# Low parts of the gate product's weights in a decoder block: ScalarE writes the negated high part, a transfer from DRAM adds the raw weights

## The chip, the core and the metric

The kernel runs on one core of a Trainium2 chip. The core has a matrix engine (TensorE, PE in the profile, with its weight loads as PEld), three engines for elementwise work (VectorE = DVE, ScalarE = ACT, GpSimd = POOL), SyncE (SP), which issues transfers, and 16 DMA engines. Each engine works through its own queue of instructions in order and waits on semaphores for the others. The metric is the device time of one execution in microseconds; smaller is better.

## The reference

The reference is one decoder block over 512 tokens of width 1024: two parallel branches (a short gated convolution and an mLSTM in chunks) from one wide input projection, a gated merge, an output projection, and at the end a gate with a per-layer embedding and a last normalisation. What matters here is the end:

```python
        merged = jax.nn.sigmoid(ga) * ya + jax.nn.sigmoid(gb) * yb
        x = x + jnp.einsum('bsd,de->bse', merged, w_o[l])

        gate = jax.nn.sigmoid(jnp.einsum('bsd,de->bse', rmsnorm(x, g_ple[l]), w_ple_gate[l]))
        x = x + gate * jnp.einsum('bsp,pd->bsd', p[l], w_ple[l])
    return rmsnorm(x, g_final)
```

The product with `w_ple_gate` (1024 x 1024, float32) is the gate product. It is the last large product of the kernel.

## The kernel before

**Precision.** Every large product is made of three: each float32 operand is cut into a high part (the operand rounded to the matrix engine's float32r format) and a low part (the operand less its high part, also in float32r), and `mm3` adds high x high (L233), high x low (L234) and low x high (L235) in PSUM. For weights, one operand is a tile of 128 x 4 x 512 numbers (2048 per partition, 1 MB). It lies raw in a tile `wraw` (four buffers), loaded by SyncE, and is cut in two halves (h = 0, 1) of 128 x 1024 each into the tiles `whi` and `wlo`. These have two buffers for each half, so that one operand can be cut while another is in use. In the profile a matmul's two inputs are named with the moving one first: `mm<-wlo,h` multiplies a low part of the weights.

**The list of operands.** `operands` lists the weight tiles in the order of their use, each with the sums that are to be made after its split: many of the kernel's products are made in Strassen's way with seven products in place of eight, and the sums of raw tiles that this needs are made by transfers that POOL issues (`add_chunk`, L156), which add a piece of DRAM weights to a raw tile in SBUF. The output projection `w_o` is such a product. The gate product is not: its four operands (two column halves n, two row halves) are the last four of the list, appended by the loop over `block(w_pg_v, ...)`, and no sum follows their split.

**The order of the work.** The order on TensorE, ScalarE, VectorE and GpSimd is that in which the code is written out. `next_operand` hands out the next operand and queues the split of the one after it; `tick`, called after each block of 12 or 24 matmuls, takes one half from that queue and calls `split_half`. So an operand's halves are cut while the operand ahead of it is in use. In `split_half` ScalarE writes the high part (L180) and VectorE subtracts it from the raw tile (L181). What a `tick` emits stands in ScalarE's and VectorE's queues behind the work of the blocks before.

**The end.** The last seven-product stage (`w_o`) runs until 795.7 us of the span. Its results are added to the residual, squared for the norm (`esq`, L1287), turned by TensorE (`ptk`, L1248) and cut (`h`, L240 and L241 or L243 and L244). Then the gate product runs in this order: first operand with token tiles 2 and 3, second operand with 2, 3, 0 and 1, first operand again with 0 and 1 (all for the first 512 columns; `gate_embedding` takes each finished tile through the sigmoid `e`, the product with the embedding and the residual `xr`, and POOL multiplies the result by the last norm's weights, `xg`, L1337). For the other 512 columns `last_part` uses the third operand with tiles 0 and 1, the fourth with 0 and 1, and then both with tiles 2 and 3. What follows each finished tile there is a long run of small steps on ScalarE, VectorE and POOL up to the output.

Of the kernel before, what the change touches and what calls it, by code (L numbers as in the profile page):

```python
# [9 lines left out]
F32 = mybir.dt.float32  # L10
F32R = mybir.dt.float32r
AF = mybir.ActivationFunctionType
ALU = mybir.AluOpType
# [23 lines left out]
def hybrid_block(ctx, tc, x, p, g_mix, w_in, conv_w, conv_b, w_a_out, b_gates, g_head,  # L37
                 w_b_out, w_o, g_ple, w_ple_gate, w_ple, g_final, out):
    nc = tc.nc
    act, dve, pool, pe = nc.scalar, nc.vector, nc.gpsimd, nc.tensor  # L40
# [28 lines left out]
    chunks, operands = [], []  # L69
# [10 lines left out]
    def block(view, pieces, halves=(0, HC)):  # L80
        for k0 in halves:
            operands.append((chunk(view, k0, pieces), []))
# [38 lines left out]
    for j, u in enumerate((b11, b21, b11, b22, b11, b12, b11)):  # L121
        for g in range(2):
# [4 lines left out]
    begun = {sums: o12}  # L127
    operands.extend([(o11, []), (sums, [(sums, o22, None)]), (o21, [(o12, o22, None)]), (sums, [(sums, o21, None)]),
                     (o22, []), (o12, []), (sums, [])])
    for n in range(2):  # L130
        block(w_pg_v, [(n * CW, CW)])

# [21 lines left out]
    def add_chunk(to, c, ks):  # L154
        for src, _, cs in chunks[c]:
            nc.gpsimd.dma_start(raws[to][:, ks, cs], src[:, ks, :], accum_op=ALU.add)  # L156
# [14 lines left out]
    def split_tiles(i, h):  # L171

        parts = [wsplit.tile([P, HH, CW], F32R, name=f"w{u}{i}{h}", tag=f"w{u}{h}", align_bytes=256)
                 for u in ("hi", "lo")]
        splits.setdefault(i, []).append(parts)
        return raws[operands[i][0]][:, HH * h:HH * h + HH, :], *parts

    def split_half(i, h, e_lo=None):
        t, hi, lo = split_tiles(i, h)
        act.activation(hi, t, AF.Copy)  # L180
        (e_lo or dve).tensor_tensor(lo, t, hi.bitcast(F32), ALU.subtract)  # L181
        ks = slice(HH * h, HH * h + HH)
        for to, c, eng in operands[i][1]:
            if eng is not None:
                eng.tensor_tensor(raws[to][:, ks, :], raws[to][:, ks, :], raws[c][:, ks, :], ALU.add)
            else:
                add_chunk(to, c, ks)
        if h == 1:
            done(i)

    def done(i):
        for c in [c for c in raws if last_use[c] == i]:
            del raws[c]
        load_free()
# [7 lines left out]
    def next_operand(follow=True):  # L202

        i = state["use"]
        state["use"] += 1
        while pieces:
            split_half(*pieces.popleft())
        if follow:
            queue_split()
        got = splits.pop(i)  # L210
        return [[got[kt // HH][u][:, kt % HH, :] for kt in range(HC)] for u in range(2)]
# [4 lines left out]
    def tick():  # L216
        new = [g for g in fresh if not next(g, True)]
        fresh.clear()
        if pieces:
            split_half(*pieces.popleft())  # L220
        active[:] = [g for g in active if not next(g, True)] + new
# [354 lines left out]
    def quarter(q):  # L576
        hi, lo = (u[:, q % HH, :] for u in splits[0][q // HH])
        return hi, lo, raws[0][:, q, :]
# [6 lines left out]
    hi, lo, raw = quarter(0)  # L585
# [47 lines left out]
    for t in range(2):  # L633
        keep_ple(t, 1, pss[t])

    split_half(1, 0, pool)
    for k in range(3):
        turn_x(k)
# [6 lines left out]
    for g in range(2):  # L645
        src = wg_raw[:, :, g * NH:(g + 1) * NH]
# [808 lines left out]
```

## Time and profile before

| | |
|---|---|
| time, median of 3 runs | 852.58 us (847.28 to 853.58) |
| the profiled execution, its own time | 851.58 us |
| its span, first to last instruction | 849.8 us |
| TensorE busy | 837.7 us (99%) |
| weight loads busy | 729.8 us (86%) |
| VectorE busy | 649.8 us (76%) |
| ScalarE busy | 498.1 us (59%) |
| GpSimd busy | 209.0 us (25%) |
| moved by DMA | 172.83 MB, mean 203 GB/s |
| transfers queued by POOL | 70.33 MB, 44.7% of the 16 engines' span |
| transfers queued by SP and ACT | 101.72 MB, 36.0% of the 16 engines' span |

Times inside the kernel are given in microseconds from the start of the span. A row of a timeline reads: start, duration, engine, line of the code, instruction, what it writes and reads, shape, count, and in brackets how long the engine had stood idle before it and what ended that. Matmuls are pipelined: a row shows 0.39 us, and one starts every 0.23 us. A row of the chain of work gives start, length, engine and line. A row of busy time by stretch gives the stretch, its length, busy time and number of instructions of TensorE, of the weight loads, of VectorE, ScalarE and POOL, the clock that TensorE was granted (1 is full speed), the share of the DMA engines that was busy, and GB/s. A row of the waits gives who waited for whom, us in total, times, and the longest.

### The profile page before, as it was taken

To read this page: it belongs to the slowest core of one execution; us is meant where nothing else is said; L and a number is where in the kernel's file an instruction comes from. 1 tells how busy PE (TensorE), PEld (TensorE's weight loads), DVE (VectorE), ACT (ScalarE), POOL (GpSimd) and SP (SyncE) were. 2 spreads that over 40 slices of the span, in tenths; PEclk is the share of its full clock that TensorE was granted. 3 is DMA by queue.
4 is the path that set the end of the run, shared out by engine and by line. 5 is a ranking of instruction groups with operands and counts; after the bars stand their busy time and mean duration, and the time that the engine had idled before them with its cause. 6 is when DMAs were issued, how large, how long until landed. Compare 5 with 4: busy or idle time off the path is not lost.

```text
span 849.8 us, 12141 instructions
## 1 busy us (share of the span) xinstructions
PE 837.7 (99%) x4602; PEld 729.8 (86%) x4602; DVE 649.8 (76%) x876; ACT 498.1 (59%) x726; POOL 209.0 (25%) x204
## 2 busy tenths in 40 slices
PE   9999999999999999999999999999999999999996
PEld 7888888888889988888888999999998887888885
DVE  5786767976787667788668779797885787899565
ACT  6467665667765576565776555545443355667543
POOL 5103122203124321220222333342410222122031
PEclk9999999999999999999999999999999999999998
DMA  9748769779968997896998799999989489799502
GB/s 316 266 139 177 163 135 222 196 267 238 266 127 207 245 223 166 200 219 208 256 230 212 161 213 181 183 182 182 182 276 375 83 199 275 195 250 228 191 0 100
DMA packets 103355, 172.83 MB, mean 203 GB/s; under 512 B 5564, under 2 KB 46064, under 8 KB 102016
## 3 DMA queue, kind: packets, MB, share of 16 engines
q0 software_dynamic: 39488, 70.33, 44.7%
q1 hardware_dynamic: 59792, 94.64, 33.7%
q10 hardware_dynamic: 4016, 7.08, 2.3%
q8 instruction: 36, 0.59, 0.3%
q14 instruction: 23, 0.19, 0.1%
HBM read 155.25 MB, written 16.78 MB: 202 GB/s over the span
## 4 chain that ended last, share of the span: by engine, by line
PE 93%; DMA 2%; DVE 2%; issue 1%; ACT 1%; SPq 0%; POOL 0%; POOLq 0%; ACTq 0%; DVEq 0%
PE mm L235 28%; PE mm L234 28%; PE mm L233 28%; DMA wraws<-in_w_b_out 2%; PE pv L233 1%; PE pv L235 1%; PE pv L234 1%; PE pty L816 1%; DMA xin<-in_x 1%; PE sc L235 1%; PE sc L234 1%; PE sc L233 1%; PE ptk L1248 0%; PE pth L1129 0%; PE pt L553 0%
## 5 line engine op out<-in xcount | busy, mean ns | idle before, releaser
L181 DVE TENSOR_TENSOR wlo<-wraw,whi 128x1024 fp32r<-128x1024 f32 x244 | 299.5, 1229 | 113.3 <-ACT whi L180 112.9
L180 ACT ACTIVATE whi<-wraw 128x1024 fp32r<-128x1024 f32 x246 | 257.2, 1054 | 109.6 <-PE mm L235 54.8
L156 POOL DMA_DIRECT2D wraw<-in_w_in x112 | 136.9, 1424 | 336.0 <-DVE wlo L181 231.1
L349 ACT ACTIVATE s<-mm 128x512 f32<-128x512 f32 x84 | 50.2, 597 | 98.1 <-PE mm L235 96.8
L233 PE MATMUL mm<-whi,hs 128*128 128x512 f32 x256 | 99.9, 390 | 0.0
L234 PE MATMUL mm<-wlo,hs 128*128 128x512 f32 x256 | 99.8, 390 | 0.0
L235 PE MATMUL mm<-whi,hs 128*128 128x512 f32 x256 | 99.7, 389 | 0.0
L233 PE MATMUL mm<-hn_hi,whi 128*128 128x256 f32 (+1 forms) x304 | 93.4, 307 | 0.0
L235 PE MATMUL mm<-hn_hi,wlo 128*128 128x256 f32 (+1 forms) x304 | 92.9, 306 | 0.0
L234 PE MATMUL mm<-hn_lo,whi 128*128 128x256 f32 (+1 forms) x304 | 92.9, 306 | 0.0
L233 PE MATMUL mm<-hs,whi 128*128 128x256 f32 x320 | 90.9, 284 | 0.0
L234 PE MATMUL mm<-hs,whi 128*128 128x256 f32 x320 | 90.5, 283 | 0.0
L235 PE MATMUL mm<-hs,wlo 128*128 128x256 f32 x320 | 90.5, 283 | 0.0
L234 PE MATMUL mm<-wlo,hn_hi 128*128 128x512 f32 x192 | 75.0, 391 | 0.0
L233 PE MATMUL mm<-whi,hn_hi 128*128 128x512 f32 x192 | 74.9, 390 | 0.0
L235 PE MATMUL mm<-whi,hn_lo 128*128 128x512 f32 x192 | 74.7, 389 | 0.0
L234 PEld LDWEIGHTS mm<-hs,whi 128*128 128x128 f32 x320 | 61.4, 192 | 0.0
L233 PEld LDWEIGHTS mm<-hs,whi 128*128 128x128 f32 x320 | 61.4, 192 | 0.0
L235 PEld LDWEIGHTS mm<-hs,wlo 128*128 128x128 f32 x320 | 61.4, 192 | 0.0
L235 PEld LDWEIGHTS mm<-hn_hi,wlo 128*128 128x128 f32 x304 | 58.1, 191 | 2.7 <-POOL wlo L181 0.2
L234 PEld LDWEIGHTS mm<-hn_lo,whi 128*128 128x128 f32 x304 | 58.1, 191 | 2.4
L233 PEld LDWEIGHTS mm<-hn_hi,whi 128*128 128x128 f32 x304 | 58.1, 191 | 2.4
(349 smaller groups left out, 1679.0 us busy)
## 6 DMA issues: line engine op xcount, KB each, us to landing
wraw<-in_w_in SPq DMA_DIRECT2D x32, 1024.0 KB, 5.5
wraw<-in_w_in POOLq DMA_DIRECT2D x52, 512.0 KB, 8.1
wraw<-in_w_in SPq DMA_DIRECT2D x48, 512.0 KB, 5.3
wraw<-in_w_in POOLq DMA_DIRECT2D x60, 256.0 KB, 5.9
wraw<-in_w_b_out SPq DMA_DIRECT2D x7, 1024.0 KB, 5.2
wraw<-in_w_b_out POOLq DMA_DIRECT2D x12, 512.0 KB, 6.5
wraw<-in_w_o SPq DMA_DIRECT2D x5, 1024.0 KB, 7.6
yt_d<-yc POOLq DMA_DIRECT2D x4, 1024.0 KB, 4.9
```

Source lines behind the costliest of these rows:

```text
L156: nc.gpsimd.dma_start(raws[to][:, ks, cs], src[:, ks, :], accum_op=ALU.add)
L180: act.activation(hi, t, AF.Copy)
L181: (e_lo or dve).tensor_tensor(lo, t, hi.bitcast(F32), ALU.subtract)
L233: pe.matmul(ps, lhsT=a[0], rhs=b[0], start=first, stop=False, **kw)
L234: pe.matmul(ps, lhsT=a[0], rhs=b[1], start=False, stop=False, **kw)
L235: pe.matmul(ps, lhsT=a[1], rhs=b[0], start=False, stop=last, **kw)
L349: act.activation(to[i], src, AF.Copy, scale=scale)
L816: pe.transpose(pts[v][:, t * P:(t + 1) * P], y[:, t, v * P:(v + 1) * P], ident)
```

## The change

```diff
@@ operands, in order of use
                      (o22, []), (o12, []), (sums, [])])
+    first_pg = len(operands)
     for n in range(2):
         block(w_pg_v, [(n * CW, CW)])

@@ split_half
         t, hi, lo = split_tiles(i, h)
         act.activation(hi, t, AF.Copy)
-        (e_lo or dve).tensor_tensor(lo, t, hi.bitcast(F32), ALU.subtract)
         ks = slice(HH * h, HH * h + HH)
+        if i >= first_pg:
+            act.activation(lo, hi.bitcast(F32), AF.Copy, scale=-1.0)
+            for src, _, cs in chunks[operands[i][0]]:
+                nc.gpsimd.dma_start(lo[:, :, cs], src[:, ks, :], accum_op=ALU.add)
+        else:
+            (e_lo or dve).tensor_tensor(lo, t, hi.bitcast(F32), ALU.subtract)
```

For the last four operands, eight halves in all, the subtraction on VectorE is gone. ScalarE, right after the high part, writes its negative into the low tile, and a transfer issued by POOL then reads the same piece of the weights (512 KB, 128 x 2 x 512 float32) from DRAM again and adds it to the low tile in SBUF. The sum is the same low part. All other operands are cut as before. Lines of the changed kernel below the first edit are one higher than before, below the second six.

ScalarE's queue around the split of the second gate operand, before:

```order
L1287 ACTIVATE esq,ess<-xr 128x512 x2
L180 ACTIVATE whi_7522<-wraw_7333 128x1024
L1258 ACTIVATE yf_6199<-ptk,prm 128x256 x4
L180 ACTIVATE whi_7543<-wraw_7333 128x1024
L240 ACTIVATE h_7485<-yf_6199 128x1024
```

and after:

```order
L1293 ACTIVATE esq,ess<-xr 128x512 x2
L181 ACTIVATE whi_7524<-wraw_7333 128x1024
L184 ACTIVATE wlo_7525<-whi_7524 128x1024
L1264 ACTIVATE yf_6199<-ptk,prm 128x256 x4
L181 ACTIVATE whi_7546<-wraw_7333 128x1024
L184 ACTIVATE wlo_7547<-whi_7546 128x1024
L246 ACTIVATE h_7487<-yf_6199 128x1024
```

One pass more stands behind each high part, ahead of whatever ScalarE had next; the numbers behind the names are buffers.

The end of POOL's queue, before, where L1313 is a power for the norm's scale, L1337 the four products `xg` and L1374 the last powers:

```order
L156 DMA wraw_6960<-in_w_o 128x2x512 x2
L1313 TENSOR_TENSOR etmp_7150<-etmp_7149,mhalf 128x4
L1337 TENSOR_TENSOR xg<-xr,gfin 128x512 x4
L1374 TENSOR_TENSOR etmp_7150<-etmp_7149,mhalf 128x1 x4
L1451 UNCONDITIONAL_BRANCH
```

and after:

```order
L186 DMA wlo_7525<-in_w_ple_gate 128x2x512
L186 DMA wlo_7547<-in_w_ple_gate 128x2x512
L1319 TENSOR_TENSOR etmp_7150<-etmp_7149,mhalf 128x4
L1343 TENSOR_TENSOR xg<-xr,gfin 128x512
L186 DMA wlo_7640<-in_w_ple_gate 128x2x512
L1343 TENSOR_TENSOR xg<-xr,gfin 128x512
L186 DMA wlo_7660<-in_w_ple_gate 128x2x512
L186 DMA wlo_7703<-in_w_ple_gate 128x2x512
L1343 TENSOR_TENSOR xg<-xr,gfin 128x512
L186 DMA wlo_7723<-in_w_ple_gate 128x2x512
L1343 TENSOR_TENSOR xg<-xr,gfin 128x512
```

Four transfers (the last two of them are the first rows) now stand ahead of the power, and the other four between the products, each of which waits for a finished token tile.

TensorE's queue at the first gate operand, with the semaphores that each row waits on, before:

```order
L233 MATMUL mm<-whi_7454,h_7336 128x512 [waits Activation_49]
L234 MATMUL mm<-wlo_7455,h_7336 128x512 [waits DVE_49]
L235 MATMUL mm<-whi_7454,h_7336 128x512
L233 MATMUL mm<-whi_7479,h_7336 128x512 [waits Activation_49]
L234 MATMUL mm<-wlo_7480,h_7336 128x512 [waits DVE_49]
```

and after:

```order
L239 MATMUL mm<-whi_7454,h_7336 128x512 [waits Activation_49]
L240 MATMUL mm<-wlo_7455,h_7336 128x512 [waits DMASW5_49]
L241 MATMUL mm<-whi_7454,h_7336 128x512
L239 MATMUL mm<-whi_7480,h_7336 128x512 [waits Activation_49]
L240 MATMUL mm<-wlo_7481,h_7336 128x512 [waits DMASW6_49]
```

The order of the matmuls is unchanged; the second and the eighth of the operand's first block of twelve, which are the first to read the two low halves, now wait for a transfer in place of VectorE.

## The prediction

> **What bounds the kernel now.** I read the chain of work that ended last first, then the waits, the busy time by stretch, and last the timeline of each engine over the final 60 us, the only place that the change touches.
>
> ```profile
> core 0: 849.8 us, clock 0.994
> PE 93%; DMA 2%; DVE 2%; issue 1%; ACT 1%; SPq 0%; POOL 0%; POOLq 0%; ACTq 0%; DVEq 0%
> 827.31 0.24 PE mm L235
> 827.58 0.70 ACT e L1326
> PEld mm L234 <- DVE wlo L181: 1.2, 4, 0.3
> ```
>
> The span is 849.8 us and 93% of its chain is matmuls. The chain runs on PE up to the matmul at 827.31 (the last that the first tile of the gate product's second half needs) and then goes through ScalarE and VectorE to the end. The last row is from the waits of the weight loads over the whole span: all low parts together held TensorE up for 1.2 us. So VectorE's low parts are hidden today, and taking them off VectorE cannot shorten the path by more than that. In the last stretch, where the change lies, no row of the waits has PE as the one that waits.
>
> The gate product uses four operands, which I call G1 to G4 in order of use, each split in halves a and b. These are the first matmuls that read each low half (L234):
>
> ```profile
> 796.78 0.40 PE L234 MATMUL mm<-wlo,h 128*128 128x512 f32 x1
> 798.15 0.39 PE L234 MATMUL mm<-wlo,h 128*128 128x512 f32 x1
> 803.12 0.40 PE L234 MATMUL mm<-wlo,h 128*128 128x512 f32 x1
> 804.49 0.39 PE L234 MATMUL mm<-wlo,h 128*128 128x512 f32 x1
> 819.45 0.39 PE L234 MATMUL mm<-wlo,h 128*128 128x512 f32 x1
> 820.80 0.39 PE L234 MATMUL mm<-wlo,h 128*128 128x512 f32 x1
> 824.88 0.39 PE L234 MATMUL mm<-wlo,h 128*128 128x512 f32 x1
> 826.25 0.39 PE L234 MATMUL mm<-wlo,h 128*128 128x512 f32 x1
> ```
>
> They are the due times: G1a 796.78, G1b 798.15, G2a 803.12, G2b 804.49, G3a 819.45, G3b 820.80, G4a 824.88, G4b 826.25. TensorE's order is fixed, so a low half that is late by some time stops everything behind it for that time. The high halves on ScalarE start here:
>
> ```profile
> 788.18 1.06 ACT L180 ACTIVATE whi<-wraw 128x1024 fp32r<-128x1024 f32 x1 [1.87 <-PE mm L235]
> 793.93 0.63 ACT L1287 ACTIVATE esq<-xr 128x512 f32<-128x512 f32 x1 [1.50 <-DVE xr L1272]
> 794.56 1.04 ACT L180 ACTIVATE whi<-wraw 128x1024 fp32r<-128x1024 f32 x1
> 799.32 1.05 ACT L180 ACTIVATE whi<-wraw 128x1024 fp32r<-128x1024 f32 x1
> 801.69 1.07 ACT L180 ACTIVATE whi<-wraw 128x1024 fp32r<-128x1024 f32 x1
> 812.62 1.06 ACT L180 ACTIVATE whi<-wraw 128x1024 fp32r<-128x1024 f32 x1 [1.18 <-PE mm L235]
> 814.20 1.05 ACT L180 ACTIVATE whi<-wraw 128x1024 fp32r<-128x1024 f32 x1
> 819.42 0.69 ACT L1326 ACTIVATE e<-mm,er 128x512 f32<-128x512 f32 x1 [2.03 <-PE mm L235]
> 820.00 1.05 ACT L180 ACTIVATE whi<-wraw 128x1024 fp32r<-128x1024 f32 x1
> 821.56 1.05 ACT L180 ACTIVATE whi<-wraw 128x1024 fp32r<-128x1024 f32 x1
> ```
>
> The eight whi rows are G1a to G4b in order. What the reader is to see is how little lies between them and the due times: from G1b's start to its use 3.6 us, from G2b's 2.8 us, from G4b's 4.7 us. A VectorE pass of 1.2 us fits into that; a transfer hardly does. And they cannot start earlier: G1b is queued behind an instruction that waits on VectorE, which waited on a matmul, and G3a and G4a stand behind waits on TensorE itself.
>
> **The change, part by part.** Eight VectorE subtractions go. They cost nothing on the path (above), so their removal gains nothing; the most it could gain is a share of that 1.2 us. Eight ScalarE passes come, SBUF to SBUF, 128x1024, like the high parts: 1.05 us each. Each also pushes what stands behind it on ScalarE by 1.05 us until ScalarE next waits for something else. Eight transfers of 512 KB come, issued by POOL, each only when its ScalarE pass has ended. The hop from an engine's end to POOL's start I read from the same kind of transfer for w_o:
>
> ```profile
> 772.19 1.22 DVE L181 TENSOR_TENSOR wlo<-wraw,whi 128x1024 fp32r<-128x1024 f32 x1
> 773.71 1.20 POOL L156 DMA_DIRECT2D wraw<-in_w_o  x1 [1.67 <-DVE wlo L181]
> ```
>
> VectorE ended at 773.41, POOL began at 773.71: 0.3 us. So a transfer is issued 1.05 + 1.05 + 0.3 = 2.4 us after its high part starts. What remains is the time from issue to landing, L. The kernel already adds 512 KB of DRAM weights to SBUF in this way, float32 to float32:
>
> ```profile
> DMA to landing us min/median/max: 4.4/6.2/13.9
> 674.71 1.19 POOL L156 DMA_DIRECT2D wraw<-in_w_b_out  x1 [7.33 <-DVE wlo L181]
> 676.59 1.19 POOL L156 DMA_DIRECT2D wraw<-in_w_b_out  x1 [0.69 <-DVE wlo L181]
> wraw<-in_w_b_out POOLq DMA_DIRECT2D x1, 512.0 KB, 5.7
> wraw<-in_w_b_out POOLq DMA_DIRECT2D x1, 512.0 KB, 6.4
> wraw<-in_w_o POOLq DMA_DIRECT2D x1, 512.0 KB, 9.2
> wraw<-in_w_o POOLq DMA_DIRECT2D x8, 512.0 KB, 8.6
> ```
>
> The first row is of all such transfers of w_in, smaller ones among them. The 5.7 belongs to a transfer issued into quiet (674.71), the 6.4 to the one 1.9 us behind it, the 9.2 to the one at 770.84 with plain loads running beside it, and 8.6 is the median of w_o's eight. Which is nearest? The DMA load of the stretch tells:
>
> ```profile
> 788.00:796.00 8.00, 8.00 (x42) 6.71 (x41) 3.52 (x5) 5.30 (x11) 0.00 (x0) 1.00 0.81 281
> 796.00:804.00 8.00, 8.00 (x44) 6.83 (x43) 5.03 (x6) 6.48 (x14) 0.00 (x0) 1.00 0.31 126
> 804.00:814.00 10.00, 10.00 (x45) 8.26 (x44) 7.67 (x17) 4.56 (x10) 3.59 (x3) 1.00 0.01 2
> ```
>
> The columns that matter are the last three: granted clock, DMA share, GB/s. G1a, issued at 790.6, falls into a busy stretch (0.81): L = 9.2. From about 800 there is next to nothing (0.01), so I take the quiet rows, 6.0 between 5.7 and 6.4, since the b halves follow their a halves by 2.6 to 3.5 us. The ends for the range are 4.4, the shortest that POOL issued to these buffers, and 8.6. That the target is now a float32r tile is shown by no row; it may cost nothing or more, which is a reason to keep the upper end.
>
> First round. G1a: 788.18 + 2.4 + 9.2 = 799.8, late by 3.0. G1b: 794.56 + 2.4 + 6.0 = 803.0, late by 4.8. G2a stands behind one added pass: 799.32 + 1.05 + 2.4 + 6.0 = 808.8, late by 5.7. G2b stands behind two: 801.69 + 2.1 + 2.4 + 6.0 = 812.2, late by 7.7. These do not add, as they start from ScalarE's queue and not from TensorE: the latest counts, 7.7, or L + 1.7.
>
> Second round. G3 and G4 start from TensorE (the waits in their rows), so they are shifted by the 7.7 and come on top. G3a: 812.62 + 2.4 + 6.0 = 821.0, late by 1.6. G3b, one pass behind: 823.7, late by 2.9. G4a: 828.4, late by 3.5. G4b, one pass behind: 821.56 + 1.05 + 2.4 + 6.0 = 831.0, late by 4.8, or L - 1.2. Again the latest counts: 4.8. Together 2 L + 0.5 = 12.5 us.
>
> Behind the waits: POOL's queue holds the power (L1313) and four products (L1337) between and behind the new transfers. The power comes behind G2b's transfer, at 807.5, but what needs it, the first sigmoids, waits for matmuls that are 7.7 us late. One product stands ahead of G4b's transfer:
>
> ```profile
> 818.92 1.30 POOL L1337 TENSOR_TENSOR xg<-xr,gfin 128x512 f32<-128x512 f32 x1 [4.55 <-DVE xr L1328]
> ACT e L1326 <- PE mml L235: 0.4, 1, 0.4
> ```
>
> After G4a's issue (822.4 + 1.2) and this 1.30 POOL is free at 824.9, and G4b is ready at 825.0: nothing, though nothing is spare either. The second row says that at the very end ScalarE still waits 0.4 us for the last matmul, so TensorE has no slack there that could swallow a shift. Bandwidth of the 4 MB costs nothing with a DMA share of 0.01.
>
> **The clock.** One stall of such a length is in the trace:
>
> ```profile
> 710.30 0.39 PE L234 MATMUL mm<-wlo,l 128*128 128x512 f32 x1
> 712.63 0.50 PE L235 MATMUL mm<-whi,l 128*128 128x512 f32 x1 [1.95 <-DVE l L1046]
> 713.95:717.36 3.41, 3.41 (x10) 2.67 (x10) 3.41 (x4) 0.00 (x0) 1.07 (x1) 0.50 0.36 93
> ```
>
> TensorE stood for 1.95 us, and 1.3 us after it went on its granted clock was 0.50 for 3.41 us: 1.7 us lost. (In this row ten matmuls fill 3.41 us.) The waits that I expect are 3.0, 1.8, 0.9 and 2.0 us, then 1.6, 1.3, 0.6 and 1.3. By that row one or two of them lower the clock, but what is lost between two waits is taken back by the next, which ends when a transfer lands; I take 0.8 us, with 0 and 3.4 as its ends. The Trainium skill, page "TensorE: Matmul & The Clock Gate", Part 1, says that the clock halves after at least one idle window of about 3.4 us. By that rule none of these waits would lower it and the sum would be 12.5 alone; the row here lowered it after 1.95 us, and I go by the row.
>
> Sum: 12.5 + 0.8 = 13.3 us. The profiled execution took 851.58 us in all, 1.8 more than its span, so 864.9, say 865; it lies 1.0 under the median of the three runs, 852.58.
>
> **The rivals.** (1) Crowded or converting transfers: L is 8.6 or more also in the quiet stretch, because it is the add into SBUF or the float32r target that is slow. For it: the spread up to 13.9. Against: 5.7 in quiet. It gives 2 x 8.6 + 0.5 + 0.8 = 18.5, so 870. (2) Short transfers: L of 4 or less, faster than any row has it; 2 x 4 + 0.5 = 8.5, so 860, and below that the change is within 1%. The 4.4 of the smallest bounds it at 861. The Trainium skill, page "DMA: Bandwidth & Descriptors", section "Anatomy of one DMA — SWDGE (gpsimd) path", gives 2.0 us plus the bytes by 436 GB/s per transfer issued by GpSimd; that is an estimate of 3.2 us for 512 KB and of 6.9 us for the sum, 858.5. No row here agrees with it; the quiet one took 5.7. (3) Not slower: the transfers are hidden. Its place is ScalarE's queue at G1b and G2b: with VectorE relieved, what they queue behind would have to end so early that they start 5 us sooner than now, at about 789.7 and 796.1. Against: what G1b stands behind is released by a matmul through VectorE, not by VectorE's load. Its time would be 852. (4) The clock stays low through the whole of the rest: two more windows of 1.7 us on the forecast, 868; the single row shows full clock after one window.
>
> **How the numbers follow.** L between 5 and 8 as forecast 0.62, crowded 0.16, short 0.13, hidden 0.03, clock 0.06. About 1% (8.5 us, from 844 to 861) is what a measurement of this kernel tells from no change. Slower by over 1%: forecast, crowded and clock, 0.84. Within 1%: short and most of hidden, 0.15. Faster: 0.01. The range leaves out the hidden case and the far ends: from 859.5, short transfers, to 873, crowded with the clock's upper end.
>
> **What would show it.** In the profile after: eight transfers into wlo from POOL with 5.7 to 6.5 us to landing (the first near 9); waits of TensorE's L234 on these transfers of about 7.7 us over G1 and G2 and 4.8 over G3 and G4; a granted clock below 1 in a window behind 797; the matmul now at 827.31 between 840 and 841; the stretch from there to the end as long as before, 22.5 us. Wrong is the forecast if the landings are far from 6, if TensorE's waits stand at other operands, or if the end does not move with that matmul.

## The result, and the profile after

| | before | after |
|---|---|---|
| median, with the runs of before taken beside it | 850.30 us (847.28 to 853.58, 4 runs) | 861.72 us (861.46 to 862.80, 4 runs) |
| time over that of before | 1 | 1.0144 (95% interval 1.0116 to 1.0172) |
| span of the profiled execution | 849.8 us | 859.4 us |
| start of G1a's high part on ScalarE | 788.18 | 784.84 |
| from there to the end of the span | 61.6 us | 74.6 us |

The changed kernel is slower by 1.4%; the forecast was 865, with 859.5 to 873 as its range. The last row is the measure that I use from here on, and I call it the tail stretch: it begins with the first instruction of the gate product's splits, the first place that the change touches. Ahead of it both kernels do the same work, but their profiled executions differ there by 3.3 us. The tail stretch grew by 12.9 us (74.56 less 61.62).

The page of after, first its busy times, then the chain of work that ended last by engine, then the row of the costliest groups for VectorE's low parts:

```profile
PE 839.3 (98%) x4602; PEld 729.3 (85%) x4602; DVE 640.5 (75%) x868; ACT 506.3 (59%) x734; POOL 217.6 (25%) x212
...
PE 91%; DMA 3%; DVE 2%; ACT 1%; issue 1%; POOL 0%; SPq 0%; POOLq 0%; ACTq 0%
...
L188 DVE TENSOR_TENSOR wlo<-wraw,whi 128x1024 fp32r<-128x1024 f32 x236 | 288.2, 1223 | 105.6 <-ACT whi L181 105.0
```

The edit did what it says: VectorE has eight instructions and 9.3 us less, ScalarE eight passes and 8.2 us more, POOL eight transfers more. In the chain TensorE has 2 points less (93% before) and the DMA engines 1 more; the rest is lost in rounding. TensorE's waits, in after, over the last 75 us (who waits for whom, us in total, times, longest):

```profile
PEld mm L240 <- DMA wlo<-in_w_ple_gate: 11.2, 6, 5.7
PE mm L240 <- DMA wlo<-in_w_ple_gate: 9.0, 5, 5.3
```

Before, no row of this stretch had TensorE as the one that waits. TensorE's timeline of after has these five waits, the only ones from 790 to 845:

```profile
798.96 0.79 PE L240 MATMUL mm<-wlo,h 128*128 128x512 f32 x1 [5.35 <-DMA wlo<-in_w_ple_gate]
825.60 0.50 PE L240 MATMUL mm<-wlo,h 128*128 128x512 f32 x1 [1.26 <-DMA wlo<-in_w_ple_gate]
828.17 0.50 PE L240 MATMUL mm<-wlo,h 128*128 128x512 f32 x1 [0.93 <-DMA wlo<-in_w_ple_gate]
833.15 0.50 PE L240 MATMUL mm<-wlo,h 128*128 128x512 f32 x1 [0.59 <-DMA wlo<-in_w_ple_gate]
835.67 0.50 PE L240 MATMUL mm<-wlo,h 128*128 128x512 f32 x1 [0.87 <-DMA wlo<-in_w_ple_gate]
```

They are the first reads of the low halves of G1a, G3a, G3b, G4a and G4b. G1b, G2a and G2b do not wait. Next, the busy time by stretch of after around the first of them; the columns are as in the prediction, the granted clock third from the end:

```profile
790.00:797.30 7.30, 3.61 (x21) 2.82 (x19) 2.33 (x3) 5.45 (x10) 1.20 (x1) 1.00 1.03 295
797.30:804.10 6.80, 5.14 (x12) 4.03 (x13) 0.73 (x1) 5.97 (x9) 2.41 (x2) 0.50 1.04 198
804.10:812.00 7.90, 7.90 (x40) 6.58 (x40) 3.86 (x13) 2.40 (x5) 1.03 (x1) 1.00 0.46 71
```

The wait for G1a is followed by a clock of one half for 6.8 us. Comparing the start of each matmul, counted from G1a's high part, with the same one of before, TensorE is 5.5 us behind at G1a, and 2.5 us more by the time the clock is back (5.14 us of work at half clock): 8.1 us for the first round. Over G3 and G4 it loses 4.8 us more. Together they are the 12.9. (The expectations below were written with 7.9 and 4.9 for the two rounds.) The four waits of the second round add up to 3.65 in the rows, but each costs some 0.3 us more than its row says: a matmul otherwise starts 0.16 us before the one ahead of it ends, which it can't do behind a wait, and the next one starts 0.33 us behind it in place of 0.23 (825.60 and 825.93).

The transfers themselves, in after: first POOL's timeline for G1a, G2b and G4b, then three rows of the DMA issues (KB each, us from issue to landing).

```profile
787.29 1.20 POOL L186 DMA_DIRECT2D wlo<-in_w_ple_gate  x1 [15.73 <-PE ptk L1254]
802.69 1.20 POOL L186 DMA_DIRECT2D wlo<-in_w_ple_gate  x1 [2.29 <-ACT wlo L184]
829.81 1.20 POOL L186 DMA_DIRECT2D wlo<-in_w_ple_gate  x1
```

```profile
wlo<-in_w_ple_gate POOLq DMA_DIRECT2D x1, 512.0 KB, 11.6
wlo<-in_w_ple_gate POOLq DMA_DIRECT2D x1, 512.0 KB, 5.9
ple<-ple_d SPq DMA_DIRECT2D x4, 512.0 KB, 8.7
```

POOL's idle time ahead of the first row is put down to `ptk`, but the pass that it waits for ended on ScalarE at 787.00, 0.3 us ahead of the issue. 11.6 is G1a's, 5.9 is G2b's, and the eight in order took 11.6, 7.7, 5.6, 5.9, 5.8, 5.7, 5.9 and 5.8. So G2b's low half landed at 802.69 + 5.9 = 808.6, and its first read is the matmul at 809.2: 0.6 us to spare, and only because TensorE was already 8.1 us late. Had TensorE kept its old pace from G1a's start on, that read would have come at 804.49 - 3.3 = 801.2, and the wait would have been 7.4. G2b's chain and G1a's wait with its half clock thus reach nearly the same lateness: the first round is set twice.

### The profile page after: what moved, and what is told of

Same layout as the page of the kernel before. It is cut to its first block, busy times and chain, and to the rows that moved or that the text cites. A ratio compares the mean times of both kernels' runs of the same rounds, so it can differ in the third digit from the quotient of the medians.

```text
span 859.4 us, 12151 instructions
## 1 busy us (share of the span) xinstructions
PE 839.3 (98%) x4602; PEld 729.3 (85%) x4602; DVE 640.5 (75%) x868; ACT 506.3 (59%) x734; POOL 217.6 (25%) x212
## 4 chain that ended last, share of the span: by engine, by line
PE 91%; DMA 3%; DVE 2%; ACT 1%; issue 1%; POOL 0%; SPq 0%; POOLq 0%; ACTq 0%
PE mm L240 28%; PE mm L241 28%; PE mm L239 28%; DMA wlo<-in_w_ple_gate 2%; PE pv L241 1%; PE pv L240 1%; PE pv L239 1%; PE pty L822 1%; DMA xin<-in_x 1%; PE sc L241 1%; PE sc L240 1%; PE sc L239 1%; PE pth L1135 0%; PE pt L559 0%; DVE xin L554 0%
## 5 line engine op out<-in xcount | busy, mean ns | idle before, releaser
L188 DVE TENSOR_TENSOR wlo<-wraw,whi 128x1024 fp32r<-128x1024 f32 x236 | 288.2, 1223 | 105.6 <-ACT whi L181 105.0
```

## The experiments

**Theory.** The added time is two rounds of low halves that land late, as the prediction has it: the first starts from ScalarE's queue and has G1a's crowded landing and G2b's chain as its two limits; the second starts from TensorE. **Rivals.** It is ScalarE's eight added passes, not the transfers; or the traffic and POOL's queue; or the clock.

All times over that of before are with their 95% intervals. "Extra" is the tail stretch less 61.6 us.

| run | median us | time over before | tail stretch | extra |
|---|---|---|---|---|
| the change | 861.72 | 1.0144 (1.0116 to 1.0172) | 74.6 | 12.9 |
| G3 and G4 only | 854.05 | 1.0044 (1.0023 to 1.0065) | 66.1 | 4.5 |
| G1 and G2 only | 859.13 | 1.0113 (1.0086 to 1.0139) | 68.9 | 7.3 |
| passes, no transfer | 853.01 | 1.0042 (1.0028 to 1.0057) | 66.1 | 4.5 |
| passes and unread transfers | 853.40 | 1.0050 (1.0034 to 1.0066) | 65.8 | 4.2 |
| G1 only | 858.23 | 1.0094 (1.0065 to 1.0123) | 70.6 | 9.0 |
| G2 only | 859.81 | 1.0123 (1.0098 to 1.0148) | 71.1 | 9.5 |
| negated on VectorE | 865.27 | 1.0180 (1.0146 to 1.0213) | 76.2 | 14.6 |
| busy wait ahead of G1 | 862.99 | 1.0155 (1.0134 to 1.0176) | 76.9 | 15.3 |
| embedding loaded early | 862.48 | 1.0153 (1.0129 to 1.0178) | 73.4 | 11.8 |
| own buffers for G3 | 859.27 | 1.0090 (1.0056 to 1.0124) | 70.1 | 8.5 |
| own buffers, G3 and G4 only | 850.15 | 1.0001 (0.9983 to 1.0020) | 61.6 | 0.0 |
| before, again | 849.06 | 1.0009 (0.9990 to 1.0028) | 61.6 | 0.0 |

### Before, again

No edit: the kernel before, as one more kernel among the others.

> The kernel before, unchanged, profiled once more: how far the stretch from G1a's high part to the end (61.6 us) and the stretch ahead of it (788.2 us) repeat by themselves. If the stretch is a sound measure: 61.6 within 0.3. The part ahead of it may differ by 3 us or more, since the profiles so far, whose code there is the same, differ by that much behind a wait of TensorE near 710 us and the half clock that followed it in some of them; ratio 0.998 to 1.002.

Its tail stretch is 846.1 - 784.50 = 61.6 us, as in the first profile of before, though the part ahead of it was 3.7 us shorter. So the tail stretch repeats far better than the whole, and the part ahead is what scatters. The prediction's quoted wait at 712.63 (1.95 us, then a half clock) is in the first profile of before; this one and that of after have no such wait.

### G3 and G4 only

```diff
-        if i >= first_pg:
+        if i >= first_pg + 2:
```

> Only the third and fourth gate operands (G3, G4) are cut the new way; G1 and G2 as before. Measured by the stretch from the start of G1a's high part to the end of the span: 61.6 us before, 74.6 with the whole change (+12.9). Theory (two rounds of landing times exposed, 7.9 and 4.9 us in the changed kernel): only the second round, +4.5 to +5.3, with TensorE's L240 waiting on transfers only at G3 and G4; time 1.005 to 1.006 of before. Rival 1 (the added ScalarE passes delay everything): half of the change, +6.5. Rival 2 (one slow first transfer and the clock behind it are all of the cost): about 0.

The second round alone: 4.5 us. TensorE's timeline in this run has these waits and no others behind 790:

```profile
819.45 0.50 PE L240 MATMUL mm<-wlo,h 128*128 128x512 f32 x1 [1.12 <-DMA wlo<-in_w_ple_gate]
822.18 0.50 PE L240 MATMUL mm<-wlo,h 128*128 128x512 f32 x1 [1.08 <-DMA wlo<-in_w_ple_gate]
826.81 0.50 PE L240 MATMUL mm<-wlo,h 128*128 128x512 f32 x1 [0.26 <-DMA wlo<-in_w_ple_gate]
829.33 0.50 PE L240 MATMUL mm<-wlo,h 128*128 128x512 f32 x1 [0.87 <-DMA wlo<-in_w_ple_gate]
```

What the reader is to see: the waits of the whole change at G3 and G4 are here again although G1 and G2 are as before. They are a round of their own, which the first neither causes nor swallows, and waits of this size left the clock at 1.00.

### G1 and G2 only

```diff
-        if i >= first_pg:
+        if first_pg <= i < first_pg + 2:
```

> Only G1 and G2 are cut the new way. Theory: only the first round, +7.2 to +8.2 in the stretch, no wait of TensorE at G3 and G4; together with the run on G3 and G4 the two add up to the whole (12.9 within 1). Rival 1: +6.5 again. Rival 2: all of it, +12.9.

The first round alone: 7.3 us. TensorE's timeline in this run has one wait:

```profile
799.91 0.80 PE L240 MATMUL mm<-wlo,h 128*128 128x512 f32 x1 [5.33 <-DMA wlo<-in_w_ple_gate]
```

Behind it the half clock lasted 3.4 us, not 6.8, which is 1.7 lost (granted clock third from the end):

```profile
799.90:803.30 3.40, 3.39 (x8) 2.66 (x9) 0.00 (x0) 3.37 (x7) 1.20 (x1) 0.50 0.98 152
```

5.33, 0.3 and 1.7 are the 7.3. The two rounds by themselves, 7.3 + 4.5 = 11.8, come within 1.1 us of the whole, where I had expected 1; the clock, 2.5 there and 1.7 here, is most of that.

### Passes, no transfer

ScalarE negates as in the change, but VectorE adds the raw tile in place of the transfer, so its eight instructions are back.

```diff
-            for src, _, cs in chunks[operands[i][0]]:
-                nc.gpsimd.dma_start(lo[:, :, cs], src[:, ks, :], accum_op=ALU.add)
+            dve.tensor_tensor(lo, t, lo.bitcast(F32), ALU.add)
```

> ScalarE writes the negated high part as in the change, but VectorE adds the raw weights in place of the transfer. Theory: the passes alone cost little, 0 to +1 in the stretch, no wait of TensorE at L240 over 0.5 us. Rival 1 (ScalarE's eight passes of 1.06 us are the cost): +8 or more.

A miss: 4.5 us, with no transfer at all. G2b's halves, on ScalarE, VectorE and TensorE in this run's timelines:

```profile
802.80 1.06 ACT L184 ACTIVATE wlo<-whi 128x1024 fp32r<-128x1024 f32 x1
803.89 1.23 DVE L185 TENSOR_TENSOR wlo<-wraw,wlo 128x1024 fp32r<-128x1024 f32 x1 [2.27 <-ACT wlo L184]
805.17 0.50 PE L239 MATMUL mm<-wlo,h 128*128 128x512 f32 x1 [1.83 <-DVE wlo L185]
```

Three added passes stand ahead of the end of G2b's low half: G1b's and G2a's ahead of its high part, which starts 2.1 us later for them, and its own between its high part and VectorE. Its cover was 2.8 us between the start of its high part and its use. VectorE's 1.23 behind three passes no longer fits. The busy time by stretch shows what followed (granted clock third from the end):

```profile
802.50:805.90 3.40, 1.57 (x7) 1.00 (x6) 2.01 (x2) 3.00 (x5) 0.00 (x0) 1.00 0.00 0
805.90:809.30 3.40, 3.40 (x10) 2.70 (x9) 2.04 (x9) 0.42 (x2) 1.03 (x1) 0.51 0.02 5
```

A wait of 1.83 us, with 0.43 at G2a, 0.3 more for each, and then 3.4 us at half clock, which is 1.7 lost: these are the 4.5. My expectation had priced the passes as if they only pushed; the pushes were in the prediction's own sum for G2b, and I did not carry them over to a kernel without transfers. The rival that the passes cost time by themselves holds, for G2b. In the full change the pushes are not a further term. They are part of G2b's chain: its high part starts 15.4 us behind G1a's there (800.23 - 784.84), 13.5 before.

### Passes and unread transfers

ScalarE's passes and the transfers write into a tile that nothing reads, and VectorE makes the low parts as before; the output doesn't depend on the eight added passes and transfers.

```diff
-            act.activation(lo, hi.bitcast(F32), AF.Copy, scale=-1.0)
+            junk = junk_pool[0].tile([P, HH, CW], F32R, ...)
+            act.activation(junk, hi.bitcast(F32), AF.Copy, scale=-1.0)
+            dve.tensor_tensor(lo, t, hi.bitcast(F32), ALU.subtract)
...
-                nc.gpsimd.dma_start(lo[:, :, cs], src[:, ks, :], accum_op=ALU.add)
+                nc.gpsimd.dma_start(junk[:, :, cs], src[:, ks, :], accum_op=ALU.add)
```

> The passes and the eight transfers stay as they are, but write to a tile of their own that nothing reads, and VectorE makes the low part as before. Theory: DMA traffic, POOL's queue and ScalarE's passes cost nothing by themselves, 0 to +1.5 in the stretch. Rival 1: +8 or more. Rival 3 (the traffic, or POOL's products behind the transfers, delay the end): +5 or more.

4.2 us, above what I expected, and at the same place: TensorE waited 1.20 us for G2b's high part, which stands behind two added passes (G1b's and G2a's), and 0.76 for its low part, and the clock was half for 3.4 us. In its timeline and ScalarE's:

```profile
803.25 0.50 PE L244 MATMUL mm<-whi,h 128*128 128x512 f32 x1 [1.20 <-ACT whi L183]
804.51 0.50 PE L245 MATMUL mm<-wlo,h 128*128 128x512 f32 x1 [0.76 <-DVE wlo L189]
799.74 1.06 ACT L188 ACTIVATE junk<-whi 128x1024 fp32r<-128x1024 f32 x1 [0.95 <-DMA junk<-in_w_ple_gate]
```

These two waits, 0.3 for each and the 1.7 lost are 4.3: nothing is left over for 4 MB of traffic and eight issues in POOL's queue, so that rival falls. But the passes and the transfers are not parted cleanly here. By the last row G2a's pass, which writes into the same scratch tile as G1a's, waited 0.95 us for G1a's transfer to land in it, and this pushed G2b too. Otherwise, what the transfers cost in the change, they cost by landing late for their reader.

### G1 only, G2 only

G1 only:

```diff
-        if i >= first_pg:
+        if i == first_pg:
```

> Only G1 is cut the new way. With G1 and G2 the stretch was +7.3 us, and TensorE waited at G1a alone (5.3 us, then a half clock for 3.41 us). Theory A (the first round is set twice: G1a's transfer is slow beside the plain loads, and G2b's would be as late): G1 alone already gives it, +6 to +7.5. Rival (the round is set by G2b, whose high part stands behind all the added passes): +2 or less.

G2 only:

```diff
-        if i >= first_pg:
+        if i == first_pg + 1:
```

> Only G2 is cut the new way. Theory A: G2b starts at 801.7 of the before time, +1.05 for one pass ahead, +2.4, +5.8 to landing = 810.95 against a due time of 804.49: +6 to +7, and with the clock up to +8. Rival (G1a's slow landing is the whole of the round): G2 alone costs at most what ScalarE's passes cost, +2 to +4.

Each half of the first round costs by itself what the round costs, and more: 9.0 and 9.5 us, beyond both expectations. The waits of TensorE in the first run, by its timeline:

```profile
801.46 0.80 PE L240 MATMUL mm<-wlo,h 128*128 128x512 f32 x1 [5.57 <-DMA wlo<-in_w_ple_gate]
```

and in the second:

```profile
806.47 0.50 PE L240 MATMUL mm<-wlo,h 128*128 128x512 f32 x1 [3.86 <-DMA wlo<-in_w_ple_gate]
810.20 0.80 PE L240 MATMUL mm<-wlo,h 128*128 128x512 f32 x1 [1.99 <-DMA wlo<-in_w_ple_gate]
```

Waits of 5.6 and of 5.9 us, and in each a half clock of 6.8 us, in the first run and then in the second:

```profile
800.80:807.60 6.80, 6.14 (x14) 4.80 (x15) 3.81 (x9) 2.64 (x5) 1.03 (x1) 0.50 0.37 67
807.90:814.70 6.80, 4.81 (x12) 3.54 (x12) 3.52 (x10) 1.55 (x3) 0.00 (x0) 0.50 0.28 53
```

The second figure of a row is TensorE's work in it, and half of that is lost. Compared matmul by matmul with before, G1 alone is 5.7 us behind at its wait and loses 3.0 more by the clock, 8.7; G2 alone is 6.4 behind at its second wait and loses 2.2 more, 8.6. The rest of the 9.0 and 9.5, 0.3 and 0.9 us, arises behind ScalarE's last instruction, in the last store of the output (4.2 and 4.9 us to the end of the span, 4.0 before), and is no cost of the round. The first is G1a's slow landing, the second G2's chain. That the two do not add (7.3 together) shows the round to be set twice; that each alone is above 7.3 comes from the clock, which cost 1.7 us in the run with both and 2.5 in the whole change.

### Embedding loaded early

G1a's transfer shares the DMA engines with the plain loads of the embedding (`ple`, 2 MB), which SP issues at the same time. Here two of the four tiles are loaded earlier by SP and two later by ScalarE's queue.

```diff
+    for i in range(2):
+        nc.sync.dma_start(ple_early[:, i, :], ple_d[:, 2 + i, :])
...
-        for t in (2, 3, 0, 1):
-            nc.sync.dma_start(u[:, t, :], ple_d[:, t, :])
+        for t in (0, 1):
+            nc.scalar.dma_start(u[:, t, :], ple_d[:, t, :])
...
-    load_ends()
...
+            if (c, t) == (1, 3):
+                load_ends()
```

> The whole change; two of the four tiles of the embedding product are loaded some 20 us earlier into a tile of their own, the other two some 20 us later from ScalarE's queue, so that they no longer run beside G1a's transfer, which took 11.6 us beside them. Theory (G2b sets the first round whatever G1a does): G1a lands in 6 to 8 us, TensorE waits at G1b, G2a and G2b instead, the stretch stays at +12 to +14. Rival (G1a's crowded landing is what the first round costs): +8 or less.

The DMA issues of this run have for G1a

```profile
wlo<-in_w_ple_gate POOLq DMA_DIRECT2D x1, 512.0 KB, 5.5
```

where it was 11.6, and less than the 6 to 8 that I expected: the neighbours were the reason for the slow landing. And the time hardly moved, 11.8 us extra and a ratio of 1.0153. TensorE did not wait at G2a and G2b, as I had expected; in its timeline the one wait of the first round stands one operand half further on, at G1b:

```profile
804.31 0.79 PE L240 MATMUL mm<-wlo,h 128*128 128x512 f32 x1 [4.14 <-DMA wlo<-in_w_ple_gate]
```

That wait, 0.3 and the half clock behind it (6.8 us, 6.2 of them at work, 3.1 lost) make 7.5; matmul by matmul the first round is 7.3, 0.8 less than in the change. So G1b is one more limit close to the others, and a single cause taken away from a round with several limits gains little.

### Negated on VectorE

```diff
-            act.activation(lo, hi.bitcast(F32), AF.Copy, scale=-1.0)
+            dve.tensor_scalar(lo, hi.bitcast(F32), -1.0, None, ALU.mult)
```

> VectorE writes the negated high part, ScalarE gets no new pass, the eight transfers stay. With ScalarE's passes and no transfer the stretch was +4.5, which I had put at 0 to +1. Theory A: the landings set the rounds, the passes only push them: first round +6 to +8 (G1a as late as before), second about 3.4 in place of 4.9 (no pass ahead of G3b and G4b), together +9.5 to +11.5. Rival (ScalarE's passes are a good part of the cost, added to the landings): 12.9 - 4.5 = +8.4 or less.

Both missed, upward: 14.6 us. G1a's transfer starts later than in the change, not sooner: its pass stands in VectorE's queue behind a residual sum that waits for TensorE. Its issue in POOL's timeline of this run:

```profile
793.31 1.20 POOL L186 DMA_DIRECT2D wlo<-in_w_ple_gate  x1 [16.50 <-DVE wlo L184]
```

This is 3.2 us after the start of its high part (790.10), where the change has 2.4 (787.29 - 784.84). G2b's transfer does start sooner, 15.7 us behind the start of G1a's high part in place of 17.9, and with a wait of 5.26 at G1a and a half clock the first round is 7.4 us, 0.7 less than in the change. It is the second round that grew, to 7.2 from 4.8: waits of 0.78 at G3a, 1.69 at G3b and 1.99 at G4b, and 3.4 us more at half clock. VectorE's passes for G3b and G4b were long, in its timeline:

```profile
824.63 2.57 DVE L184 TENSOR_SCALAR wlo<-whi 128x1024 fp32r<-128x1024 f32 x1 [0.87 <-ACT whi L181]
832.00 2.90 DVE L184 TENSOR_SCALAR wlo<-whi 128x1024 fp32r<-128x1024 f32 x1 [0.48 <-ACT whi L181]
```

The other six took 0.7 us. GpSimd ran a product `xg` beside both of these (824.88 and 832.58, 1.77 us each); whether that made them long was not tried. So ScalarE as the place of the pass isn't what makes the change slow.

### Busy wait ahead of G1

22 matmuls are put ahead of the gate product's first, to keep TensorE working until G1a's low half lands; their result is thrown away.

```diff
+            if (c, t) == (0, 2):
+                for _ in range(22):
+                    pe.matmul(pss[t], lhsT=lhs_x(t, 0)[0], rhs=w[c][0][0], start=True, stop=True)
```

> The whole change, and 22 matmuls whose result is thrown away ahead of G1's first, where TensorE waited 5.3 us: they fill the wait and hold the clock up. Theory (the clock's loss of 2.4 us in the first round is mostly cover for G2b, which lands only 0.8 us ahead of its use): the stretch falls from +12.9 to +11.4 to +12.4, and TensorE waits 1 to 2 us at G2b instead. Rival (the clock's loss is added in full): +10.5. If the matmuls are no cover but work: +13 to +18.

TensorE's timeline in this run, the 22 and then two of the first reads of low halves (G1a and G2b):

```profile
793.53 5.25 PE L1360 MATMUL mm<-whi,h 128*128 128x512 f32 x22
...
799.50 0.50 PE L240 MATMUL mm<-wlo,h 128*128 128x512 f32 x1 [0.49 <-DMA wlo<-in_w_ple_gate]
...
810.60 0.50 PE L240 MATMUL mm<-wlo,h 128*128 128x512 f32 x1 [2.13 <-DMA wlo<-in_w_ple_gate]
```

and its busy time by stretch behind the second:

```profile
807.70:811.10 3.40, 1.27 (x6) 0.77 (x5) 1.25 (x3) 0.87 (x2) 0.00 (x0) 1.00 0.16 27
811.10:814.50 3.40, 3.40 (x9) 2.65 (x9) 1.03 (x2) 0.69 (x1) 0.00 (x0) 0.50 0.00 0
```

It worked where it was put: the clock stayed at 1.00 through G1, and the waits there shrank to 0.49 and 0.66. But G2b now was the late one, and its wait of 2.13 lowered the clock after all. The cost is 15.3 us extra, worse than the change. That lies in my range for matmuls that are no cover but work, yet they were cover, since G1a's first low read is 5.7 us behind that of before with them and 5.5 in the change. The rival (the clock is a separate cost that can be taken out) isn't borne out, as G2b stops TensorE also when the clock has stayed up. My own 11.4 to 12.4 missed, because G2b's landing took 7.5 us here and 5.9 in the change, and why is not shown; SP issued no plain loads beside it. With 5.9 it would have landed at 809.0, 0.5 us behind the start of that wait (808.47): an estimate. What a busy wait saves with such a landing stays open.

### Own buffers for G3

G3 starts late because its tiles are those of G1, and because it is queued only when G2 is used up. Here its halves get buffers of their own, it is cut one operand earlier, and G4 takes G2's buffers.

```diff
+        if own and i == first_pg + 2:
+            parts = own[h]
...
-            w[c] = next_operand(len(w) == 0)
+            w[c] = next_operand()
```

> The whole change, and G3 is cut one operand earlier into buffers of its own, so that its transfers are issued about 10 us ahead of the due time, and G4 takes G2's buffers as soon as they are free. Same passes, same eight transfers. Theory (only what is issued too late costs): no wait at G3 and G4, the second round goes, +7 to +9 is left in the stretch. Rival (passes, traffic or POOL's queue cost by themselves): +12 to +13.

8.5 us extra. TensorE's timeline from 790 to 845 has a single wait, and G3 and G4 have none:

```profile
801.51 0.80 PE L245 MATMUL mm<-wlo,h 128*128 128x512 f32 x1 [5.35 <-DMA wlo<-in_w_ple_gate]
```

The second round is gone, as expected; the first stays. No run here gives G1 and G2 more lead.

### Own buffers, G3 and G4 only

The same, with `if i >= first_pg + 2:` so that only G3 and G4 are made in the new way.

> Only G3 and G4 are cut the new way (+4.5 in the stretch with the old buffers), with G3 a step earlier in buffers of its own. Theory: the transfers are hidden, 0 to +0.7, no wait of TensorE on a transfer, time 0.998 to 1.002 of before. Rival: +3 or more.

The first of G3's transfers in POOL's timeline, and the first read of that tile in TensorE's:

```profile
804.71 1.23 POOL L191 DMA_DIRECT2D own_lo<-in_w_ple_gate  x1
...
817.64 0.39 PE L245 MATMUL mm<-own_lo,h 128*128 128x512 f32 x1
```

12.9 us lie between them, and the landing took 5.5. The extra is 0.0 and the ratio 1.0001 (0.9983 to 1.0020). With enough lead, the new way of making the low parts costs nothing; and with four subtractions fewer on VectorE it also gains nothing. No version here beats the kernel before.

## Why the prediction was right

**The direction, and why.** Right: TensorE's fixed order stops at the first reads of low halves that land late, and taking the subtractions off VectorE gives nothing back. The run with the lead restored and the time of before shows both.

**The two rounds.** Right: 7.7 and 4.8 in the forecast (12.5), with 0.8 for the clock 13.3; 8.1 (clock included) and 4.8 in the trace, 12.9 in the tail stretch. The second round is right place by place: 1.6, 2.9, 3.5 and 4.8 us late at its four reads in the forecast, 1.4, 2.7, 3.6 and 4.7 in the trace. G3 and G4 alone cost 4.5, and own buffers take that round away. The stretch from the sigmoid that follows the matmul at 827.31 to the end is as long as before, 22.2 us (849.8 - 827.58 and 859.4 - 837.13). I had put that matmul between 840 and 841; it came some 3.3 us sooner, as the part ahead of the tail stretch was shorter by that much.

**The terms of the first round.** Right in sum, not in place, and that the sum holds is partly luck. I had G1a, G1b, G2a and G2b late by 3.0, 4.8, 5.7 and 7.7, with waits at all four and G2b as the one that counts. By their issues and landings they were late by 5.5, 6.5, 5.0 and 7.4 against the due times of before, counted from G1a's high part. But TensorE waited at G1a alone, 5.35 us, and with the half clock behind it, which I had not put there, that covers all the others. The mis-sized terms are the landings of G1: the 9.2 of w_o's transfer stood for a stretch with a DMA share of 0.81, and G1a's measured 11.6; the 6.0 for G1b measured 7.7, still beside the plain loads. With the embedding moved both took 5.5. That G1a with its half clock came to 8.1, and G2b's chain to 7.4, is a coincidence of size: without G2b as a second limit the error at G1a would have been one of the sum.

**The quiet landing.** 6.0 forecast, 5.6 to 5.9 measured for the six transfers behind G1. In other runs single transfers of G2 took 7.2 to 7.8 with no plain load issued beside them, and why is not shown. The float32r target, which no row of before showed, adds nothing to the 5.7 of the quiet float32 transfer. The Trainium skill, page "DMA: Bandwidth & Descriptors", section "Anatomy of one DMA — SWDGE (gpsimd) path", would give an estimate of 3.2 us by its 2.0 us plus bytes by 436 GB/s; none of the low parts' transfers agrees, the shortest in any of these runs being 5.3.

**The clock.** 0.8 forecast, with 3.4 as its end. Behind G1a's wait the clock lost 2.5 us in the profiled execution, 1.7 to 3.0 in the other runs with that wait. I took what it loses to be regained at the next wait. In the trace there was no next wait until G3, but the argument holds in another way: without the loss TensorE would have waited for G2b until it was 7.4 us late, 7.7 with the 0.3 behind a wait, so that by this estimate only some 0.4 of the 8.1 is added by the clock.

**The total.** 864.9 was made on an execution of 851.58, whose part ahead of the tail stretch was 3.3 us longer than that of after. This scatter, not the sum, makes up most of the 3.2 us between forecast and median; it is also the likely reason why the medians differ by 11.4 us where the tail stretch differs by 12.9, since the runs of before lie 6.3 us apart.

**The chances.** The hidden rival got 0.03; it is true of a kernel with more lead, not of this one.

## What to carry to other kernels

Before an elementwise step on the path to a matmul is replaced by a pass and a transfer, subtract for each tile the start of its split from its first read. The transfer needs that lead (here 2.4 us to the issue and mostly 5.3 to 6.0 us from there to the landing, 7.2 to 7.8 in single cases, and up to 11.8 beside plain loads), and a tile without it stops the matrix engine. Where several tiles are late from the same queue, their lateness does not add, and curing one shows the next; where a later round starts from the engine that waits, its lateness comes on top. Compare kernels on the stretch that the edit can touch (for the kernel before it repeated to 0.02 us while the whole scattered by over 3). In a kernel that stalls even that stretch isn't exact: the same first wait cost 1.7 to 3.0 us of clock.

## What the runs showed of the hardware

**The clock drops on short waits, and not always; windows of 3.41 us decide.** Waits of 1.95 us (before), 1.83 us (VectorE adding) and 2.13 us (busy wait) were each followed by 3.4 us at half clock. The Trainium skill, page "TensorE: Matmul & The Clock Gate", Part 1, gives at least one idle window of about 3.4 us as the condition; these three waits don't agree. But one of 2.31 us did not lower it, and neither did one of 2.92. In the timelines and the busy time by stretch of the kernel with G3 and G4 only, then of the one with G2 only:

```profile
713.00 0.50 PE L241 MATMUL mm<-whi,l 128*128 128x512 f32 x1 [2.31 <-DVE l L1052]
713.56 0.50 PE L241 MATMUL mm<-whi,l 128*128 128x512 f32 x1 [2.92 <-DVE l L1052]
```

```profile
713.90:717.30 3.40, 3.40 (x17) 2.76 (x16) 3.40 (x4) 0.32 (x1) 0.65 (x1) 1.00 0.33 55
715.70:719.10 3.40, 3.40 (x16) 2.81 (x16) 3.40 (x4) 1.27 (x2) 1.23 (x1) 1.00 0.61 182
```

Ahead of the last matmul of the gate product all drops lasted 3.4 or 6.8 us, and in each trace they lie on a grid: in the kernel negated on VectorE the half clock begins at 712.62, 801.37 and 842.33 us, 88.75 and 40.96 apart, which is 26 and 12 times 3.413. Laid over the waits, this grid tells the cases apart:

| kernel | wait, us | its parts in windows of the grid | clock behind it |
|---|---|---|---|
| before | 1.95 | 1.95 | half for one window |
| passes, no transfer | 1.83 | 1.83 | half for one |
| G3 and G4 only | 2.31 | 0.58, 1.73 | full |
| G2 only, near 713 | 2.92 | 1.68, 1.24 | full |
| G1 and G2 only | 5.33 | 1.91, 3.41, 0.01 | half for one |
| the change | 5.35 | 0.30, 3.41, 1.64 | half for two |
| own buffers for G3 | 5.35 | 1.30, 3.41, 0.64 | half for two |

So what counts is the idle time within one window. From 690 us to the last matmul of the gate product, in the traces of all these kernels, every window with 1.95 us or more of such idle time was followed by half clock and none with 1.77 or less; between them 1.83 lowered the clock, 1.87 and 1.91 did not. Once low, the clock came back behind a window with at most 0.01 us of it, and stayed low for one window more behind one with 0.62 or more. This is read off these traces; no run moved a wait on purpose. What it means for a forecast: TensorE loses half of what it works at half clock, and the same wait of about 5.35 us cost 1.7 us of clock in one run, 2.5 in the change and 3.0 in a third, as its end fell in the grid.

**An accumulating transfer shares with plain loads.** G1a's 512 KB took 11.6 us beside SP's loads of the embedding (8.7 us each) and 5.5 without them.
